# Head norms, gain factors and gate tiles of the query-key-value stage, rearranged

## The chip, the cores and the metric

The kernel is one program on one core of a Trainium2 chip. The core has five engines with an instruction queue each: TensorE (PE; its weight loads are listed as PEld), VectorE (DVE), ScalarE (ACT), GpSimd (POOL) and SyncE (SP), which here only starts transfers. Each queue is worked off in order, and an instruction that has to wait holds back all that stands behind it. The metric is the device time of one launch in microseconds (us), the median of several runs. "Faster" and "slower" are against the kernel before.

## The reference

A trunk of two layers on x (1024 tokens, width 1024, all float32): layer 0 is RWKV-7 time mixing and an MLP; from its output shared keys, values and forget gates are made; layer 1 is causal attention with 16 heads of 64 and an MLP. The part that the change touches is this one:

```
def shared_kv(x, kv_norm_g, kv_w, kv_f_bias, k_norm_g):
    h = rmsnorm(x, kv_norm_g)
    proj = h @ kv_w                                   # keys | values | 16 forget logits
    k = to_heads(proj[..., :D]); v = to_heads(proj[..., D:2 * D])
    f_logit = (proj[..., 2 * D:] + kv_f_bias)
    k = rmsnorm(k, k_norm_g)                          # per head, 64 wide
    c = cumsum(log_sigmoid(f_logit))
...
    q = rmsnorm(to_heads(h @ w_q), q_norm_g)          # h = rmsnorm(x, attn_norm_g)
    logits = q k^T / 8 + (c[t] - c[s]);  causal softmax;  p v;  @ w_o
```

## The kernel before, in words

**Where the stage stands.** `stage_qkv` follows the first MLP and runs in the profile from about 1393 us to 1676 us; `stage_attention` follows it. The normalised x is kept feature-first in blocks of 512 features by 512 tokens (B11, B21 for the first 512 tokens, B12, B22 for the others). The norm gains `kv_norm_g` and `attn_norm_g` are multiplied into the rows of the weights (`scale_on`, L72, called at L1579). Each float32 operand is split into a high and a low part (`wh`/`wl` for weights, `xh`/`xl` for x), and three products of parts make one float32 product.

**Six jobs of 512 output columns.** Keys, queries and values of the lower 512 columns, then of the upper 512. The first job (keys) is done plainly: for each half of the tokens, 96 matmuls into four banks of PSUM (`plain`), then `leave` copies the four banks to two tiles C on ScalarE. The other five jobs go through `proj_seven`, a Strassen-Winograd scheme with seven products A11, A12, S1, S2, S3, A22, S4 of 48 matmuls each. It needs sums of x blocks (T1 to T4, formed in place over the raw blocks B11 and B21 in `Operands.forms` and `forms2`, on VectorE with casts on ScalarE) and sums of weight blocks (`form`). Four of the seven products give a tile C, 512 tokens by 256 columns.

**What follows a C.** For keys and queries, `heads_T(...).emit` first makes the head norms: on ScalarE a square (`hsq`, L1675), on VectorE a sum over 64 (`hss`, L1676), then `rsqrt_small` (L79 to L91: VectorE, two steps on ScalarE, four on VectorE, on small tiles of 128x16), then a multiplication of C in place (L1680). The four transposes and their way to memory (`turn`, L1683: transpose on TensorE, `ht` with the head gain on ScalarE at L1690, a store from SP at L1691) come later: `emit` puts `turn` in the list `later` with a count of 4, and `tick()`, called once per product, lets it run when the count is used up. `tick(2)` between the two halves of the plain job takes two off the first half's count.

**Buffers.** PSUM has eight banks, all with the tag `mm`: a product of `proj_seven` takes two, a group of the plain job four, one `turn` two. C has three places, `ht` two, each part of weights (`wh`, `wl`) four.

**Attention.** Heads go in pairs. For each pair, `load` fetches keys and queries (`raw`), the cumulated gates of two heads spread over all partitions (`b<-d_c`, L1899, three places), and GpSimd makes of each a masked copy (`dg`, L1914, pool `t_d` with three places). `scores` (L1804, L1808, VectorE) adds `dg` and `b` to the products of TensorE and takes the row extreme; ScalarE then takes the exponential.

**What sets the order.** The framework's scheduler writes out one static order per engine from the program's order, priorities and a model of times; a tile can be placed in memory as soon as what lay there is done with. So an edit here can move instructions that it doesn't name.

Of the kernel before, what the change touches and what calls it, by code (L numbers as in the profile page):

```python
# [8 lines left out]
F32 = mybir.dt.float32  # L9
F32R = mybir.dt.float32r  # L10
AF = mybir.ActivationFunctionType
ALU = mybir.AluOpType
AX = mybir.AxisListType
# [3 lines left out]
P = 128  # L17
# [3 lines left out]
N = 64  # L21
NK = D // P
C = 64
# [29 lines left out]
    "q": {"n0": "vvvv", "n1": "vvsvvvvv", "r": "ssssssssssssssss", "Bh": "vvvvvvvv", "Bl": "vpvpvpvp", "t1": "ppvv",  # L53
        "t2": "vvvv", "t3": "vpvv", "t4": "vvvv", "T1h": "ssss", "T1l": "pppp", "T2h": "ssss", "T2l": "vpvv", "T3h":
        "spvv", "T3l": "vpvp", "T4h": "ssss", "T4l": "vpvp", "B22h": "vsss", "B22l": "vvpp", "wh": "spspsssssssvss",
        "wl": "vpvpvpvvvvpvpv", "wf": "pvvvvpvv", "wg": "vvvpvvsvvvvvssss"},
}


# [12 lines left out]
def scale_on(k, e, out, x, col):  # L72
    if e == "s":
        k.nc.scalar.mul(out, x, col)
    else:
        engine(k, e).tensor_scalar(out, x, col, None, op0=ALU.mult)
# [1493 lines left out]
def proj_seven(k, ps, p0, p1, p2, pool, w_tile, tick, X, w, gain, emit, number):  # L1570

    nc = k.nc
    A = {}
    for h in range(2):
        t = w_tile()
        nc.sync.dma_start(t, w[512 * h:512 * h + 512].rearrange("(k p) e -> p k e", p=P))
        for i in range(NK // 2):
            g = gain[:, 4 * h + i:4 * h + i + 1]
            scale_on(k, ENG["q"]["wg"][8 * number + 4 * h + i] if number < 2 else "v", t[:, i], t[:, i], g)  # L1579
        A[f"A1{h + 1}"], A[f"A2{h + 1}"] = t[:, :, 0:256], t[:, :, 256:512]  # L1580

    def form(dst, x, y, op):
        e = ENG["q"]["wf"][4 * number + "S1 S2 S3 S4".split().index(an)] if number < 2 else "v"
        engine(k, e).tensor_tensor(A[dst], A[x], A[y], op=op)

    U, V = (p2.tile([P, 2, 512], F32, tag=t, name=t, bufs=1) for t in ("U", "V"))
    for q, (an, bn) in enumerate([("A11", "B11"), ("A12", "B21"), ("S1", "T1"), ("S2", "T2"), ("S3", "T3"),
                                  ("A22", "T4"), ("S4", "B22")]):
        if an == "S1":
            A["S"] = pool().tile([P, NK // 2, 256], F32, tag="S", name="S", bufs=1)  # L1590
            form("S", "A21", "A22", ALU.add)
        elif an == "S2":
            form("S", "S", "A11", ALU.subtract)
        elif an == "S3":
            form("A21", "A11", "A21", ALU.subtract)
        elif an == "S4":
            form("S", "A12", "S", ALU.subtract)
        src = A[an if an[0] == "A" else "A21" if an == "S3" else "S"]
        wh, wl = (p.tile([P, NK // 2, 256], F32R, tag=t, name=t, bufs=4) for p, t in ((p0, "wh"), (p1, "wl")))
        es = (ENG["q"]["wh"][7 * number + q], ENG["q"]["wl"][7 * number + q]) if number < 2 else ("s", "vp"[q % 2])  # L1600
        split(k, None, src, None, *(engine(k, e) for e in es), dst=(wh, wl))
        o = [ps.tile([P, 512], F32, tag="mm", name="mm") for _ in range(2)]
        for t in range(4):
            ts = slice(t * P, t * P + P)
            for i in range(NK // 2):
                xh, xl = X[bn][i]
                for m, (x, y) in enumerate(((xh, wh), (xh, wl), (xl, wh))):
                    k.pe.matmul(o[t // 2][:, 256 * (t % 2):256 * (t % 2) + 256], x[:, ts], y[:, i],
                                     start=t % 2 == 0 and i == 0 and m == 0,
                                     stop=t % 2 == 1 and i == NK // 2 - 1 and m == 2)  # L1610
        C = None if an in ("A11", "S1", "S2") else pool().tile([P, 2, 512], F32, tag="C", name="C", bufs=3)
        for b in range(2):
            if an == "A11":
                nc.scalar.copy(U[:, b], o[b])
            elif an == "S1":
                nc.scalar.copy(V[:, b], o[b])
            elif an == "S2":
                nc.vector.tensor_tensor(U[:, b], U[:, b], o[b], op=ALU.add)
                nc.gpsimd.tensor_tensor(V[:, b], V[:, b], U[:, b], op=ALU.add)
            else:  # L1620
                nc.vector.tensor_tensor(C[:, b], (V if an in ("S3", "S4") else U)[:, b], o[b], op=ALU.add)
            if an == "S3":
                nc.vector.tensor_tensor(U[:, b], U[:, b], o[b], op=ALU.add)
        tick()
        if C is not None:
            emit(*{"A12": (0, 0), "S3": (1, 1), "A22": (1, 0), "S4": (0, 1)}[an], C)
# [20 lines left out]
def stage_qkv(k, a, xt, xs, raw, p0, W, late):  # L1647
    nc, tc, ps = k.nc, k.tc, k.ps
    with ExitStack() as ctx:
# [3 lines left out]
        pool, wn, later = None, 2, []  # L1653
# [12 lines left out]

        def heads_T(dst, gcol, f0):

            def emit(fh, th, Cb):
                with tc.high_priority(offset=PRIO):  # L1670
                    ss = sp.tile([P, 2, 8], F32, tag="hss", name="hss")
                    o3 = [Cb[:, b].rearrange("p (h n) -> p h n", n=N) for b in range(2)]
                    for b in range(2):
                        sq = pool.tile([P, 8, N], F32, tag="hsq", name="hsq", bufs=1)
                        nc.scalar.activation(sq, o3[b], AF.Square)  # L1675
                        nc.vector.tensor_reduce(ss[:, b], sq, axis=AX.X, op=ALU.add)  # L1676
                    rs = sp.tile([P, 2, 8], F32, tag="hrs", name="hrs")
                    rsqrt_small(k, sp, rs, ss, 1.0 / N, 1e-6)
                    for b in range(2):
                        nc.vector.tensor_tensor(o3[b], o3[b], rs[:, b].unsqueeze(2).broadcast_to([P, 8, N]), op=ALU.mult)  # L1680

                def turn():
                    for j in range(2):  # L1683
# [5 lines left out]
                        t = pool.tile([P, 512], F32, tag="ht", name="ht")  # L1689
                        nc.scalar.mul(t, tp, gcol[:, f // P:f // P + 1])  # L1690
                        nc.sync.dma_start(dst[f:f + P, 512 * th:512 * th + 512], t)  # L1691
                later.append([4, turn])
            return emit

        def tokens(dst, f0):
# [16 lines left out]
        w, gain, emit = jobs.pop(0)  # L1712
# [10 lines left out]
        wl, U = None, p2.tile([P, 2, 512], F32, tag="U", name="U", bufs=1)  # L1723
# [13 lines left out]
                                    stop=h == 1 and i == NK // 2 - 1 and n == 2)  # L1737

        def leave(th, o):
            C = [pool.tile([P, 2, 512], F32, tag="C", name="C", bufs=3) for _ in range(2)]  # L1740
            for t in range(4):
                for fh in range(2):
                    nc.scalar.copy(C[fh][:, t // 2, 256 * (t % 2):256 * (t % 2) + 256], o[t][:, 256 * fh:256 * fh + 256])
            for fh in range(2):
                emit(fh, th, C[fh])
        o = [mm("mm") for _ in range(4)]
        plain(0, 0, o)
        X.second(xt, lambda: mm("tp"))
# [6 lines left out]
        o = [mm("mm") for _ in range(4)]  # L1755
# [12 lines left out]
def stage_attention(k, a, op):  # L1768
# [3 lines left out]
    wo = op.tile([P, D], F32, name="aw")  # L1772
    with ExitStack() as ctx:
        lp, pp, vp, dp, bp, kp, kk = (ctx.enter_context(tc.tile_pool(name="t_" + n, bufs=b, reuse_waits="tile"))
                                      for n, b in (("l", 4), ("p", 2), ("v", 2), ("d", 3), ("b", 3), ("k", 2), ("kk", 2)))
        sp = ctx.enter_context(tc.tile_pool(name="t_s", bufs=6, reuse_waits="tile"))
        ps_s = ctx.enter_context(tc.tile_pool(name="t_ps", bufs=2, space=PSUM, reuse_waits="tile"))
        ps_t = ctx.enter_context(tc.tile_pool(name="t_pt", bufs=3, space=PSUM, reuse_waits="tile"))
# [313 lines left out]
```

## Time and profile before

| what | value |
|---|---|
| median of 3 runs | 2641.9 us (2640.52 to 2645.92) |
| profiled execution | 2639.1 us, of which the span from first to last instruction is 2637.4 us |
| TensorE busy / VectorE busy / ScalarE busy | 96% / 70% / 47% of the span |
| granted TensorE clock, mean | 0.983 |

A row of the timeline has start, length, engine, line, operation, output<-input, shape and count; in square brackets the idle time of the engine just before it and who ended it. A row of the windows has the stretch, its length, then busy time and count of instructions per engine, the granted clock of TensorE as a share of the full one, the share of the transfer engines and the rate.

### The profile page before, as it was taken

How to read it: one execution, taken by the hardware profiler on the slowest of the kernel's cores; microseconds unless marked ns; L12 is line 12 of the kernel's file. 1: busy time of each engine (PE TensorE's matmuls, PEld its weight loads, DVE VectorE, ACT ScalarE, POOL GpSimd, SP SyncE). 2: the span in 40 equal slices, each digit the busy share in tenths (PEclk: the TensorE clock that was granted, in tenths of full speed). 3: DMA queues.
4: the chain of work that ended last, by engine and by line, in shares of the span. 5: the costliest groups of instructions: out<-in, count | busy, mean ns of one | idle time of the engine just before them, and what ended most of it. 6: DMA issues, size and time to landing. Idle time of an engine off the chain costs nothing.

```text
span 2637.4 us, 44718 instructions
## 1 busy us (share of the span) xinstructions
PE 2537.5 (96%) x17601; PEld 2141.5 (81%) x17601; DVE 1852.2 (70%) x2982; ACT 1237.6 (47%) x2136; POOL 507.5 (19%) x395
## 2 busy tenths in 40 slices
PE   7999998799999999999999899999999999999999
PEld 4887897677778888888888899887887888878887
DVE  6665965788868777566778768587736877746675
ACT  4763324422355555443455424588715555543332
POOL 2011222866620000000301122344300000000020
PEclk9999999899999999999999999999999999999999
DMA  4468654966425544666641321755341644376664
GB/s 129 126 168 189 169 131 145 231 162 164 114 66 164 169 139 160 250 227 240 229 147 65 118 76 64 209 137 148 87 152 48 208 163 144 131 264 220 224 212 141
DMA packets 413510, 417.51 MB, mean 158 GB/s; under 512 B 189482, under 2 KB 297218, under 8 KB 413300
## 3 DMA queue, kind: packets, MB, share of 16 engines
q1 hardware_dynamic: 394068, 392.50, 49.0%
q0 software_dynamic: 4128, 12.66, 1.3%
q10 hardware_dynamic: 15104, 9.51, 1.2%
q8 instruction: 138, 2.26, 0.4%
q14 instruction: 72, 0.59, 0.1%
HBM read 292.76 MB, written 121.82 MB: 157 GB/s over the span
## 4 chain that ended last, share of the span: by engine, by line
PE 69%; DVE 15%; DMA 6%; issue 4%; ACT 3%; POOL 2%; SPq 1%; POOLq 0%; DVEq 0%; ACTq 0%
PE mm L365 34%; PE mm L768 7%; PE mm L766 7%; PE mm L767 7%; PE mm L824 4%; PE tp L368 2%; PE wo L365 1%; DVE Tb L316 1%; DMA b<-d_c 1%; PE s L365 1%; DVE Tm L314 1%; PE z1p L1001 1%; DVE AE L427 1%; PE o L365 1%; DMA R<-d_sm 1%
## 5 line engine op out<-in xcount | busy, mean ns | idle before, releaser
L365 PE MATMUL mm<-ol,oh 128*128 128x512 f32 x896 | 349.9, 391 | 1.3 <-DVE ol L733 1.3
L365 PE MATMUL mm<-oh 128*128 128x512 f32 x896 | 349.7, 390 | 1.3 <-ACT oh L730 1.3
L365 PE MATMUL mm<-oh,ol 128*128 128x512 f32 x896 | 349.9, 390 | 0.5 <-DVE ol L733 0.3
L730 ACT CAST oh<-ra 128x1024 fp32r<-128x1024 f32 x108 | 113.8, 1054 | 335.8 <-PE mm L365 237.5
L733 DVE TENSOR_TENSOR ol<-ra,oh 128x1024 fp32r<-128x1024 f32 x108 | 137.8, 1276 | 123.6 <-ACT oh L730 123.4
L365 PEld LDWEIGHTS mm<-ol,oh 128*128 128x128 f32 x896 | 168.9, 188 | 36.9 <-DVE ol L733 1.7
L365 PEld LDWEIGHTS mm<-oh,ol 128*128 128x128 f32 x896 | 168.9, 188 | 36.5 <-DVE ol L733 1.4
L365 PEld LDWEIGHTS mm<-oh 128*128 128x128 f32 x896 | 168.8, 188 | 36.5 <-ACT oh L730 1.7
L766 PE MATMUL mm<-xhT,ah 128*128 128x512 f32 x448 | 174.3, 389 | 0.0
L767 PE MATMUL mm<-xlT,ah 128*128 128x512 f32 x448 | 174.3, 389 | 0.0
L768 PE MATMUL mm<-xhT,al 128*128 128x512 f32 x448 | 174.3, 389 | 0.0
L1495 POOL DMA_DIRECT2D xt<-d_xh x8 | 4.4, 552 | 755.1 <-DMA rb<-in_mlp_w_out_dram 421.4
L730 ACT CAST ah<-w 128x512 fp32r<-128x512 f32 x128 | 79.3, 621 | 113.5 <-PE mm L767 102.1
L766 PE MATMUL mm<-xhB,ah 128*128 128x512 f32 x336 | 130.7, 389 | 0.0
L767 PE MATMUL mm<-xlB,ah 128*128 128x512 f32 x336 | 130.7, 389 | 0.0
L768 PE MATMUL mm<-xhB,al 128*128 128x512 f32 x336 | 130.7, 389 | 0.0
L733 DVE TENSOR_TENSOR ol<-rb,oh 128x1024 fp32r<-128x1024 f32 x92 | 120.8, 1313 | 2.1 <-ACT oh L730 1.8
L1811 ACT ACTIVATE l<-l,mx 128x512 f32<-128x512 f32 (+7 forms) x128 | 99.2, 776 | 34.3 <-DVE mx L1808 34.1
L1268 ACT ACTIVATE z<-z 128x512 f32<-128x512 f32 x112 | 70.8, 633 | 68.9 <-DVE z L1265 67.3
L767 PEld LDWEIGHTS mm<-xlT,ah 128*128 128x128 f32 x448 | 84.1, 188 | 17.6
L730 ACT CAST oh<-rb 128x1024 fp32r<-128x1024 f32 x92 | 96.4, 1048 | 4.0 <-DMA rb<-in_mlp_w_out_dram 4.0
L768 PEld LDWEIGHTS mm<-xhT,al 128*128 128x128 f32 x448 | 84.1, 188 | 17.4
(487 smaller groups left out, 6952.6 us busy)
## 6 DMA issues: line engine op xcount, KB each, us to landing
rb<-in_mlp_w_out_dram SPq DMA_DIRECT2D x124, 512.0 KB
ra<-d_H SPq DMA_DIRECT2D x108, 512.0 KB
w<-in_mlp_w_in_dram SPq DMA_DIRECT2D x64, 512.0 KB
d_H<-z SPq DMA_DIRECT2D x56, 512.0 KB
d_H<-sums SPq DMA_DIRECT2D x32, 768.0 KB
raw<-in_rwkv_w_rkv_dram SPq DMA_DIRECT2D x24, 512.0 KB
KRz<-d_KR SPq DMA_DIRECT2D x16, 512.0 KB
KRz<-d_BK SPq DMA_DIRECT2D x16, 512.0 KB
```

The source lines that it names most:

```text
L314: nc.vector.tensor_tensor(Tm[:, :, 0:n, 0:m], Nb[:, :, j, j + 1:32].unsqueeze(3).broadcast_to(S), Tb[:, :, j:j + 1, 0:m].broadcast_to(S), ...
L316: nc.vector.tensor_tensor(Tb[:, :, j + 1:32, 0:m], Tb[:, :, j + 1:32, 0:m], Tm[:, :, 0:n, 0:m], op=ALU.add)
L365: return self.tc.keep_in_program_order(self.tc.nc.tensor.matmul(*args, **kw))
L368: return self.tc.keep_in_program_order(self.tc.nc.tensor.transpose(*args))
L730: nc.scalar.copy(hi, src)
L733: lo_eng.tensor_tensor(lo, src, hi.bitcast(F32), op=ALU.subtract)
L766: te.matmul(out, ah, bh, start=i == 0, stop=False)
L767: te.matmul(out, ah, bl, start=False, stop=False)
L768: te.matmul(out, al, bh, start=False, stop=i == n - 1)
L824: nc.tensor.matmul(o[e][half], wt[:, i % 4, es], xs[i][part][:, 512 * half:512 * half + 512], start=i == 0 and wt is hi and part == 0, sto ...
L1268: nc.scalar.activation(x, x if o is None else o, AF.Relu)
L1811: nc.scalar.activation(l, l, AF.Exp, bias=m, scale=-1.0, accum_out=SM[:, j, qb:qb + 1])
```

## The change

1. **One root for two C.** In the plain job the head norms of the two C of a token half are made together: `norm([C0, C1])` with tiles of 128x32 and one `rsqrt_small`, where there were two of 128x16. It is called from `leave`; `emit` then only files the turns.
2. **C over a raw block.** The two C of the second token half lie no longer in the pool of C but in one tile with the tag `KRz0`, the place of raw block B11, which is free once the form T3 has been split.
3. **Later turns.** The turns of the plain job get the counts 5 (first half) and 6 (second half) in place of 4.
4. **Gain factors on ScalarE.** All factors of weights run on ScalarE: the four of job 2's first half and the eight of each of the jobs 3 to 6, 36 in all, leave VectorE. Four were on ScalarE already.
5. **Gates' places.** The pool `t_d` of attention has four places in place of three, which also shifts what lies behind it in memory, the tiles `b` among it.

What it does to the order is shown at three places. First, TensorE after the plain job. xhB_13663 is block B21 (product A12); in the first piece, of before, xhT_13938 is T1 (product S1).

```order
L365 MATMUL mm<-wh,xhB_13663 128x256
L365 MATMUL mm<-wl,xhB_13663 128x256
L365 MATMUL mm<-wh,xlB_13664 128x256
L368 MATMUL tp<-ident,C 128x128 x16
L365 MATMUL mm<-wh,xhT_13938 128x256
L365 MATMUL mm<-wl,xhT_13938 128x256
L365 MATMUL mm<-wh,xlT_13939 128x256
```

In the change's order xhT_13927 is T1 and xhT_13935 is T2 (product S2):

```order
L365 MATMUL mm<-wh,xhT_13927 128x256
L365 MATMUL mm<-wl,xhT_13927 128x256
L365 MATMUL mm<-wh,xlT_13928 128x256
L368 MATMUL tp<-ident,C 128x128 x16
L365 MATMUL mm<-wh,xhT_13935 128x256
L365 MATMUL mm<-wl,xhT_13935 128x256
L365 MATMUL mm<-wh,xlT_13936 128x256
```

The sixteen transposes of the first half move one product back. Those of the second half stood after S2; they stand now after A22, two products later, in one group of 24 with the eight of product A12.

Second, VectorE where the second half's C are multiplied (L1680 before, L1681 now). Of before, twelve rows from factors of a later job's weights on; the last multiplication that the transposes need follows five rows further down. L1584 is a weight sum, L1621 and L1618 take products out of PSUM:

```order
L76 TENSOR_SCALAR w<-w,cols_443 128x512 x4
L1676 TENSOR_REDUCE hss<-hsq 128x8
L733 TENSOR_TENSOR wl<-S,wh 128x1024
L88 TENSOR_TENSOR rs_t<-rs_v,hrs 128x16
L1618 TENSOR_TENSOR U<-U,mm 128x512
L1676 TENSOR_REDUCE hss<-hsq 128x8
L1584 TENSOR_TENSOR S<-w 128x1024
L89 TENSOR_TENSOR rs_t<-rs_t,hrs 128x16
L85 TENSOR_SCALAR rs_v<-hss 128x16
L1618 TENSOR_TENSOR U<-U,mm 128x512
L1584 TENSOR_TENSOR w<-w 128x4x256
L90 TENSOR_SCALAR rs_t<-rs_t 128x16
```

Now:

```order
L1621 TENSOR_TENSOR C<-U,mm 128x512
L1677 TENSOR_REDUCE hss<-hsq 128x8
L88 TENSOR_TENSOR rs_t<-rs_v,hrs 128x32
L89 TENSOR_TENSOR rs_t<-rs_t,hrs 128x32
L90 TENSOR_SCALAR rs_t<-rs_t 128x32
L91 TENSOR_TENSOR hrs<-hrs,rs_t 128x32
L1677 TENSOR_REDUCE hss<-hsq 128x8
L1681 TENSOR_TENSOR C<-C,hrs 128x512 x4
L85 TENSOR_SCALAR rs_v<-hss 128x16
L733 TENSOR_TENSOR wl<-S,wh 128x1024
L1584 TENSOR_TENSOR S<-w 128x1024
L1618 TENSOR_TENSOR U<-U,mm 128x512
```

The factors are gone from VectorE, and the multiplication of the second half's C stands ahead of the next job's weight sum; before, its last part stood behind it.

Third, SP ahead of attention. Of before, from the last stores of the values (`d_v<-C`):

```order
L1698 DMA d_v<-C 128x4x256
L1893 DMA raw<-d_r 64x1024
L1899 DMA b<-d_c 128x1024 x2
L1901 DMA V<-d_v 128x8x128
L1698 DMA d_v<-C 128x4x256
L1899 DMA b<-d_c 128x1024
L1901 DMA V<-d_v 128x8x128
L1927 DMA aw<-in_attn_w_o_dram 128x1024
```

Now the same loads (L1909) stand ahead of the last six stores of queries and of all `raw`:

```order
L1696 DMA d_k<-ht 128x512 x6
L1696 DMA d_r<-ht 128x512 x2
L1909 DMA b<-d_c 128x1024 x3
L1696 DMA d_r<-ht 128x512
L1704 DMA d_v<-C 128x4x256
L1696 DMA d_r<-ht 128x512
L1903 DMA raw<-d_k 64x1024 x4
```

The three gate loads go from the end of the stage's transfers to a place ahead of sixteen loads of keys and queries. On GpSimd, on the other hand, nothing of this stage moves.

The diff:

```
@@ table ENG, stage "q" @@
-        "wl": "vpvpvpvvvvpvpv", "wf": "pvvvvpvv", "wg": "vvvpvvsvvvvvssss"},
+        "wl": "vpvpvpvvvvpvpv", "wf": "pvvvvpvv", "wg": "ssssssssssssssss"},
@@ proj_seven @@
-            scale_on(k, ENG["q"]["wg"][8 * number + 4 * h + i] if number < 2 else "v", t[:, i], t[:, i], g)
+            scale_on(k, ENG["q"]["wg"][8 * number + 4 * h + i] if number < 2 else "s", t[:, i], t[:, i], g)
@@ stage_qkv, heads_T @@
-            def emit(fh, th, Cb):
+            def norm(Cs):
                 with tc.high_priority(offset=PRIO):
-                    ss = sp.tile([P, 2, 8], F32, tag="hss", name="hss")
-                    o3 = [Cb[:, b].rearrange("p (h n) -> p h n", n=N) for b in range(2)]
-                    for b in range(2):
+                    n = len(Cs)
+                    o3 = [C[:, b].rearrange("p (h n) -> p h n", n=N) for C in Cs for b in range(2)]
+                    ss = sp.tile([P, 2 * n, 8], F32, tag=f"hss{n}", name="hss")
+                    for o, s in zip(o3, range(2 * n)):
                         sq = pool.tile([P, 8, N], F32, tag="hsq", name="hsq", bufs=1)
-                        nc.scalar.activation(sq, o3[b], AF.Square)
-                        nc.vector.tensor_reduce(ss[:, b], sq, axis=AX.X, op=ALU.add)
-                    rs = sp.tile([P, 2, 8], F32, tag="hrs", name="hrs")
-                    rsqrt_small(k, sp, rs, ss, 1.0 / N, 1e-6)
-                    for b in range(2):
-                        nc.vector.tensor_tensor(o3[b], o3[b], rs[:, b]..., op=ALU.mult)
+                        nc.scalar.activation(sq, o, AF.Square)
+                        nc.vector.tensor_reduce(ss[:, s], sq, axis=AX.X, op=ALU.add)
+                    rs = sp.tile([P, 2 * n, 8], F32, tag=f"hrs{n}", name="hrs")
+                    rsqrt_small(k, sp, rs, ss, 1.0 / N, 1e-6, tag=f"{n}")
+                    for o, s in zip(o3, range(2 * n)):
+                        nc.vector.tensor_tensor(o, o, rs[:, s]..., op=ALU.mult)
+
+            def emit(fh, th, Cb, wait=4, normed=False):
+                if not normed:
+                    norm([Cb])
...
-                later.append([4, turn])
+                later.append([wait, turn])
+            emit.norm = norm
@@ stage_qkv, leave @@
-            C = [pool.tile([P, 2, 512], F32, tag="C", name="C", bufs=3) for _ in range(2)]
+            if th:
+                C2 = k.rz.tile([P, 2, 2, 512], F32, tag="KRz0", name="C")
+            C = [C2[:, fh] if th else pool.tile([P, 2, 512], F32, tag="C", name="C", bufs=3) for fh in range(2)]
...
+            emit.norm(C)
             for fh in range(2):
-                emit(fh, th, C[fh])
+                emit(fh, th, C[fh], 5 + th, True)
@@ stage_attention @@
-                      for n, b in (("l", 4), ("p", 2), ("v", 2), ("d", 3), ("b", 3), ("k", 2), ("kk", 2)))
+                      for n, b in (("l", 4), ("p", 2), ("v", 2), ("d", 4), ("b", 3), ("k", 2), ("kk", 2)))
```

More of the change, by code (lines that the diff above doesn't have):

```diff
@@ L1667, in heads_T @@
         def heads_T(dst, gcol, f0):
-            def emit(fh, th, Cb):
+            def norm(Cs):
                 with tc.high_priority(offset=PRIO):
-                    ss = sp.tile([P, 2, 8], F32, tag="hss", name="hss")
-                    o3 = [Cb[:, b].rearrange("p (h n) -> p h n", n=N) for b in range(2)]
-                    for b in range(2):
+                    n = len(Cs)
+                    o3 = [C[:, b].rearrange("p (h n) -> p h n", n=N) for C in Cs for b in range(2)]
+                    ss = sp.tile([P, 2 * n, 8], F32, tag=f"hss{n}", name="hss")
+                    for o, s in zip(o3, range(2 * n)):
                         sq = pool.tile([P, 8, N], F32, tag="hsq", name="hsq", bufs=1)
-                        nc.scalar.activation(sq, o3[b], AF.Square)
-                        nc.vector.tensor_reduce(ss[:, b], sq, axis=AX.X, op=ALU.add)
-                    rs = sp.tile([P, 2, 8], F32, tag="hrs", name="hrs")
-                    rsqrt_small(k, sp, rs, ss, 1.0 / N, 1e-6)
-                    for b in range(2):
-                        nc.vector.tensor_tensor(o3[b], o3[b], rs[:, b].unsqueeze(2).broadcast_to([P, 8, N]), op=ALU.mult)
+                        nc.scalar.activation(sq, o, AF.Square)
[3 more added lines that the diff above has]
+                    for o, s in zip(o3, range(2 * n)):
+                        nc.vector.tensor_tensor(o, o, rs[:, s].unsqueeze(2).broadcast_to([P, 8, N]), op=ALU.mult)
+            def emit(fh, th, Cb, wait=4, normed=False):
+                if not normed:
+                    norm([Cb])
                 def turn():
```

## The prediction, made before the changed kernel ran

> **What bounds the kernel now.** I read the page's busy shares first, then the windows by stage, then the rows of TensorE that have idle time.
>
> ```profile
> span 2637.4 us, 44718 instructions
> PE 2537.5 (96%) x17601; PEld 2141.5 (81%) x17601; DVE 1852.2 (70%) x2982; ACT 1237.6 (47%) x2136; POOL 507.5 (19%) x395
> ```
>
> TensorE is busy for 96% of the span, so only what lets it stand still, or slows its clock, can be won. In windows over the stage of the change and the start of attention (stretch, length, then busy time of PE, PEld, DVE, ACT, POOL; then granted clock):
>
> ```profile
> 1410.00:1430.00 20.00, 20.00 (x90) 16.55 (x89) 20.00 (x26) 10.56 (x20) 0.00 (x0) 1.00 0.00 1
> 1430.00:1450.00 20.00, 20.00 (x128) 18.21 (x127) 19.90 (x28) 11.67 (x22) 5.74 (x2) 1.00 0.00 1
> 1450.00:1470.00 20.00, 16.41 (x138) 15.93 (x136) 18.47 (x32) 11.62 (x23) 3.63 (x2) 1.00 0.53 178
> 1470.00:1490.00 20.00, 15.40 (x118) 15.09 (x119) 15.25 (x29) 6.01 (x11) 4.52 (x2) 0.83 0.09 34
> 1490.00:1510.00 20.00, 20.00 (x170) 20.00 (x169) 15.41 (x26) 8.69 (x16) 4.36 (x2) 1.00 0.26 87
> 1680.00:1710.00 30.00, 27.74 (x236) 23.79 (x236) 23.65 (x81) 23.28 (x56) 11.44 (x7) 0.89 0.57 169
> 1710.00:1911.00 201.00, 191.55 (x1897) 164.61 (x1894) 156.75 (x519) 157.13 (x398) 81.88 (x45) 1.00 0.46 123
> ```
>
> VectorE is full from 1410 to 1450 us while TensorE is full too; then TensorE falls short by 8.2 us from 1450 to 1490, and VectorE is the engine that is behind. ScalarE is at about half all along. From 1490 on TensorE is full again. TensorE's rows with idle time, and one ahead of them (in brackets: the wait before the row and who ended it):
>
> ```profile
> 1451.90 1.03 PE L368 MATMUL tp<-ident,C 128*128 128x128 f32 x8
> 1453.79 1.09 PE L368 MATMUL tp<-ident,C 128*128 128x128 f32 x8 [0.85 <-ACT ht L1690]
> 1474.60 2.15 PE L368 MATMUL tp<-ident,C 128*128 128x128 f32 x8 [7.34 <-DVE C L1680]
> 1676.77 0.94 PE L365 MATMUL s<-K,Q 128*128 128x512 f32 x4 [0.18 <-DVE C L1621]
> 1680.70 1.05 PE L365 MATMUL s<-K,Q 128*128 128x384 f32 x4 [2.99 <-DVE mx L1804]
> 1683.11 1.83 PE L365 MATMUL s<-K,Q 128*128 128x384 f32 x4 [1.36 <-DVE mx L1804]
> ```
>
> The first three stand in the stage of the change: transposes of the plain job's C, without a wait, waiting for a free bank (0.85) and for the last multiplication of C (7.34). The others are the start of attention. After the long waits the clock is down (windows of TensorE alone: busy, granted clock, transfers):
>
> ```profile
> 1475.00:1477.00 2.00, 2.00 (x11) 0.50 0.00 0
> 1477.00:1479.00 2.00, 2.00 (x16) 0.85 0.68 257
> 1682.00:1684.00 2.00, 0.89 (x3) 0.60 1.11 370
> 1684.00:1686.00 2.00, 2.00 (x9) 0.50 0.80 280
> 1686.00:1688.00 2.00, 2.00 (x10) 0.50 0.08 31
> 1688.00:1690.00 2.00, 2.00 (x12) 0.69 0.00 0
> ```
>
> So each stall costs its own length and, behind it, some us of work at half speed.
>
> **The change part by part.** *Later turns.* A product of 48 matmuls takes 5.75 us:
>
> ```profile
> 1507.70 5.75 PE mm L365 x48
> ```
>
> The second half's transposes go from behind S2 to behind A22, 2 x 5.75 = 11.5 us of TensorE's work later; the wait for them is 7.34 us. That alone covers it, if VectorE does not come later than now. What VectorE does before that point:
>
> ```profile
> 1457.34 1.68 DVE L76 TENSOR_SCALAR w<-w,cols 128x512 f32<-128x512 f32 x4 [0.19 <-DMA w<-in_kv_w_dram]
> 1471.29 1.23 DVE L90 TENSOR_SCALAR rs_t<-rs_t 128x16 f32<-128x16 f32 x1
> 1473.86 1.29 DVE L1680 TENSOR_TENSOR C<-C,hrs 128x512 f32<-128x512 f32 x2
> L76 DVE TENSOR_SCALAR w<-w,cols 128x512 f32<-128x512 f32 x36 | 15.6, 494 | 8.4 <-DMA w<-in_kv_w_dram 4.5 <-DMA w<-in_attn_w_q_dram 3.1 <-ACT xhT L69 0.7
> L90 DVE TENSOR_SCALAR rs_t<-rs_t 128x16 f32<-128x16 f32 x16 | 9.9, 618 | 0.3
> L74 ACT ACTIVATE w<-w,cols 128x512 f32<-128x512 f32 x4 | 2.6, 714 | 5.7 <-DMA w<-in_attn_w_q_dram 5.7
> ```
>
> *Gain factors.* Sixteen of the 36 factors (four groups) stand ahead of that multiplication: 4 x 1.68 = 6.7 us that VectorE no longer has there. *One root.* Two of the four root chains of the plain job go; the three middle steps of a chain are tiny but take up to 1.23 us when GpSimd is at work (618 ns mean), so 1 to 3 us more. And the multiplication now stands ahead of the weight sums L1584 that wait for a later job's weights. VectorE should have the second half's C done near 1460 us, and TensorE, unstalled, comes for them at 1451.9 (end of A12, before the first turns) + 1.8 (first turns) + 4 x 5.75 = 1476.7: some 16 us of slack. Of the 24 transposes the last eight need product A12's C. Its root now stands on ScalarE behind four factors that wait for weights:
>
> ```profile
> 1455.88 0.44 SPq L1576 DMA_DIRECT2D w<-in_kv_w_dram  x1
> 1462.91 1.28 DVE L76 TENSOR_SCALAR w<-w,cols 128x512 f32<-128x512 f32 x3 [0.51 <-DMA w<-in_kv_w_dram]
> ```
>
> These land at 1462.9, ScalarE takes 2.6, and VectorE then has a weight sum, two copies, the root's rest and C, about 6 us: 1472, needed at 1478.5. 6 us of slack. Gain of the long wait: 7.34.
>
> *C over the raw block.* Now the second half's copies out of PSUM wait for a C place, held by the first half until its transposes:
>
> ```profile
> 1442.60 1.21 DVE L1164 TENSOR_TENSOR xlT<-raw,xhT 128x1024 fp32r<-128x1024 f32 x1
> 1453.64 1.18 ACT L1743 COPY C<-mm 128x256 f32<-128x256 f32 x4
> 1458.83 1.27 ACT L1690 ACTIVATE ht<-tp,cols 128x512 f32<-128x512 f32 x2 [2.90 <-DMA d_k<-ht]
> ```
>
> They come at 1453.64, 13 us after the plain job's last matmul (1451.9 - 2 x 5.75 = 1440.4), and hold four of eight banks; that is the 0.85. Over KRz0 they can run once T3 is split, at 1443.8 now (first row), so the banks are free when S1 wants them. Gain 0.85. The third row is a price of the other sign: `ht` has two places, and a third `ht` waits 2.9 us for a store. The group of 24 makes six `ht` in a row, so ScalarE can stand twice for some 3 us; behind it stand casts of weights, which run up to four products (23 us) ahead, and squares whose C are wanted three products later. I put it at 0; without that cover it is 2 x 2.9 = 5.8.
>
> *The clock behind it.* 2 us at 0.50, 2 at 0.85 and 0.4 us before them at half: 1.0 + 0.3 + 0.2 = 1.5. Sum of the stage: 7.34 + 0.85 + 1.5 = 9.7, between 0 and 9.7. The other factors (20 of 36, in jobs 4 to 6) and the longer time on ScalarE (36 x 714 = 25.7 us where VectorE took 36 x 494 = 17.8) lie beside a TensorE that is full; 0 both ways unless ScalarE becomes the bound (below).
>
> *Gates' places.* What the first scores wait for:
>
> ```profile
> 1628.11 18.47 SPq L1691 DMA_DIRECT2D d_r<-ht  x3
> 1671.92 2.48 SPq L1899 DMA_DIRECT2D b<-d_c  x2
> 1678.25 1.10 POOL L1914 TENSOR_SCALAR_AFFINE_SELECT dg<-b 128x1024 f32<-128x1024 f32 x1 [9.00 <-DMA b<-d_c]
> 1680.67 1.09 POOL L1914 TENSOR_SCALAR_AFFINE_SELECT dg<-b 128x1024 f32<-128x1024 f32 x1 [1.32 <-DMA b<-d_c]
> 1675.93 0.69 DVE L1621 TENSOR_TENSOR C<-V,mm 128x512 f32<-128x512 f32 x1 [2.19 <-PE mm L365]
> 1679.38 0.29 DVE L1804 CUSTOM_DVE_ANT_0 l<-s,dg 128x128 f32<-128x128 f32 x1 [2.76 <-POOL dg L1914]
> 1681.79 0.29 DVE L1804 CUSTOM_DVE_ANT_0 l<-s,dg 128x128 f32<-128x128 f32 x1 [1.24 <-POOL dg L1914]
> ```
>
> The loads are issued at 1671.9, land six to eight us later, GpSimd waits 9.00 for them, and VectorE and TensorE behind it. In the new order they stand between the stores of the row at 1628, so about 1630 to 1647, 25 us earlier; GpSimd is free for `dg` from 1669.2 (1678.25 - 9.00). Then VectorE starts when it has the last C out, 1676.6, not at 1679.38, and does the two heads without the pause, 1.2 us each (1681.79 - 1.24 - 1679.38): 1679.0. TensorE's second four of unit two start at 1679.1, not 1683.11: 4.0 us. The clock, if it holds, gives back 0.9 x 0.4 + 4 x 0.5 + 2 x 0.31 = 3.0, but VectorE has 23.65 us of work in the 30 us after 1680, against 78% later (156.75 of 201), so it would become the bound; I take half, 1.5. Sum 5.5, between 0 (loads late all the same) and 7.0. [...]
>
> **The sum.** 9.7 + 5.5 = 15.2. The profiled execution took 2639.1 (span 2637.4 and 1.7 around it): 2623.9. The median of the runs is 2.8 above it: 2641.9 - 15.2 = 2626.7, so **2627**.
>
> **The rivals.** *The start of attention stays* (chance 0.11): another late load (V, the last keys) ends last in place of the gates; for it, the transfer engines are full at 1682 (1.11). Against it, keys and queries of the first pair are loaded before. 2641.9 - 9.7 = 2632. *The stage's wait only moves* (0.11): the group of 24 waits for A12's C, or for banks, as long as before, and only attention gains: 2641.9 - 5.5 = 2636. Against it stand the 6 us of slack. *Both stay* (0.11): a gain under 5 us, 2639; also the case that the change doesn't do what it says. *ScalarE becomes the bound* (0.07), on the slower side: in each half job it now waits in its queue for weights (VectorE's 8.4 us of waits move to it) and then needs 2.6 us, nine lumps of about 3.5 us, with copies out of PSUM behind them. If TensorE finds the banks full each time, 9 x 3.5 = 31 us come in and 2641.9 - 15.2 + 31 = 2658; it decides from five lumps of nine on (17 us against 15.2). Against it: 11.62 of 20 us busy, a product lasts 5.75, and its banks are wanted again only three products on. [...]
>
> **How the numbers follow.** The forecast holds 0.60. Its own spread, 2622 to 2631, is the bounds of its terms (2641.9 - 16.7 = 2625) and the spread of three runs (2640.5 to 2645.9). To leave out no more than 2 in 10 it must take in the first two rivals: **2621 to 2637**. A difference under 0.2% (5.3 us) can't be told from none: faster 0.60 + 0.11 + 0.11 = 0.82, same 0.11, slower 0.07.
>
> **What would show it.** Right: no row of TensorE with over 1 us of idle time between 1440 and 1490, clock 1.00 in its windows, the 24 transposes in one piece; VectorE below 18 of 20 us from 1430 to 1450; `b<-d_c` issued before the first `raw`, `dg` without a wait for it, the first scores' gaps under 0.5 us. Wrong: transposes that wait for C or `ht`, matmuls that wait for ScalarE's copies, a gap of over 2 us at the first scores with another load as its end.

## The result, and the profile after

| | before | changed |
|---|---|---|
| median of 6 runs, us | 2641.83 | 2624.64 |
| profiled execution's span, us | 2637.4 | 2621.6 |
| first matmul of the stage to first scores, us | 282.82 | 272.45 |
| first scores to the fourth group of `o<-pt,V` (32 matmuls), us | 28.53 | 22.97 |

The changed kernel is faster: ratio 0.9937, 95% interval 0.9917 to 0.9957, so 17.2 us between the medians; 2627 was forecast. Two executions far off all others, one of `gates_only` (6393 us) and one of `turns_and_gates` (3571 us), are in no ratio of this document. The last two rows are differences of start times: 1392.91, 1675.73 and 1704.26 us in the trace of before, and in that of the changed kernel those of these rows:

```profile
1393.54 0.39 PE L365 MATMUL mm<-wh,xhB 128*128 128x512 f32 x1
1665.99 0.86 PE L365 MATMUL s<-K,Q 128*128 128x512 f32 x4
1688.96 1.97 PE L365 MATMUL o<-pt,V 128*64 128x128 f32 x32
```

In the profiled executions the stage of queries and keys gave 10.4 us and the start of attention 5.6; the span is 15.8 shorter, since the stage began 0.6 later and all that follows is 0.5 shorter. The changed kernel's page:

```profile
span 2621.6 us, 44704 instructions
PE 2531.6 (97%) x17601; PEld 2135.2 (81%) x17601; DVE 1837.4 (70%) x2936; ACT 1260.4 (48%) x2168; POOL 508.4 (19%) x395
```

Its windows over the same stretches (length, busy PE, PEld, DVE, ACT, POOL, then granted clock, transfers):

```profile
1430.00:1450.00 20.00, 20.00 (x124) 18.03 (x123) 17.53 (x23) 13.26 (x24) 5.20 (x2) 1.00 0.00 1
1450.00:1470.00 20.00, 20.00 (x171) 20.00 (x170) 18.01 (x29) 13.27 (x24) 6.13 (x3) 1.00 0.46 158
1470.00:1490.00 20.00, 20.00 (x171) 20.00 (x171) 18.63 (x34) 12.06 (x21) 5.06 (x3) 1.00 0.21 79
```

TensorE is full from 1430 to 1490 and its clock whole, where before it lacked 8.2 us and the clock fell to 0.83. VectorE is still at 18 of 20 us there from 1450 on. Rows of the timeline, engine by engine: the turns of the plain job, the two multiplications of C that the second group needs, ScalarE's last copies of the second half and an `ht` that waits, then the gates' loads, `dg`, and the first scores:

```profile
1458.62 1.91 PE L368 MATMUL tp<-ident,C 128*128 128x128 f32 x16
1477.63 2.78 PE L368 MATMUL tp<-ident,C 128*128 128x128 f32 x24
1457.83 2.49 DVE L1681 TENSOR_TENSOR C<-C,hrs 128x512 f32<-128x512 f32 x4
1468.41 2.39 DVE L1681 TENSOR_TENSOR C<-C,hrs 128x512 f32<-128x512 f32 x2
1442.05 0.65 ACT L1752 COPY C<-mm 128x256 f32<-128x256 f32 x2
1481.64 1.33 ACT L1695 ACTIVATE ht<-tp,cols 128x512 f32<-128x512 f32 x2 [0.49 <-DMA d_k<-ht]
1628.92 1.28 SPq L1909 DMA_DIRECT2D b<-d_c  x3
1659.46 2.15 POOL L1924 TENSOR_SCALAR_AFFINE_SELECT dg<-b 128x1024 f32<-128x1024 f32 x2
1667.02 0.94 PE L365 MATMUL s<-K,Q 128*128 128x512 f32 x4 [0.18 <-DVE C L1621]
1668.32 2.16 PE L365 MATMUL s<-K,Q 128*128 128x384 f32 x8 [0.35 <-DVE mx L1814]
1672.47 0.33 PE L368 MATMUL tp<-ident,l 128*128 128x128 f32 x1 [1.00 <-ACT pt L1838]
```

The 24 transposes start without a wait, 17.3 us after the second half's C are done (1457.83 + 2.49 = 1460.32), and run in one piece. The second half's last copies out of PSUM start at 1442.05, not at 1453.64. The gates' loads are issued 37 us ahead of the first scores (1665.99), where before it was 4 us; `dg` has no wait for them, and the two gaps of 2.99 and 1.36 us at the first scores have become 0.35. A new short wait has come, 1.00 us for the copy of `pt`.

### The profile page after: what moved, and what is told of

Its sections match the earlier page's. It is cut to its first block, busy times and chain, and to the rows that moved or that the text cites. A ratio compares the mean times of both kernels' runs of the same rounds, so it can differ in the third digit from the quotient of the medians.

```text
span 2621.6 us, 44704 instructions
## 1 busy us (share of the span) xinstructions
PE 2531.6 (97%) x17601; PEld 2135.2 (81%) x17601; DVE 1837.4 (70%) x2936; ACT 1260.4 (48%) x2168; POOL 508.4 (19%) x395
## 4 chain that ended last, share of the span: by engine, by line
PE 76%; DVE 11%; DMA 4%; issue 4%; ACT 3%; POOL 1%; SPq 1%; ACTq 0%; POOLq 0%; DVEq 0%
PE mm L365 38%; PE mm L767 7%; PE mm L766 7%; PE mm L768 7%; PE mm L824 5%; PE tp L368 2%; PE wo L365 2%; PE s L365 1%; PE o L365 1%; PE z1p L1001 1%; DVE Tm L314 1%; DVE Tb L316 1%; DMA b<-d_c 1%; DVE AE L427 1%; PE sums L201 1%
## 5 line engine op out<-in xcount | busy, mean ns | idle before, releaser
L766 PEld LDWEIGHTS mm<-xhT,ah 128*128 128x128 f32 x448 | 84.1, 188 | 17.4
```

Of the source, the lines that this page charges most:

```text
L766: te.matmul(out, ah, bh, start=i == 0, stop=False)
```

## The experiments

All ratios are to the kernel before, timed beside it, with 95% intervals. "Stage" and "start" are the two stretches of the table above, from each run's own trace. Where the long wait is there, the stage scatters: 282.82, 284.27 and 284.08 us in three kernels with the same order in it. Where neither it nor a wait for a bank of PSUM is left, the stage lies between 272.1 and 273.0 in six kernels; with the later turns alone, where waits for a bank stay, it is 274.5. Without the gates' edit the start lies between 26.3 and 28.5, though these kernels were not changed there: a difference of 2 us in the start isn't the gates' edit by itself.

| run | ratio | stage | start |
|---|---|---|---|
| gates_only | 0.9979 (0.9971 to 0.9988) | 284.27 | 22.97 |
| room_without_fourth_gate | 0.9983 (0.9972 to 0.9993) | 284.08 | 22.97 |
| all_but_gates | 0.9956 (0.9943 to 0.9970) | 272.45 | 26.47 |
| factors_only | 0.9994 (0.9983 to 1.0006) | 281.87 | 27.14 |
| raw_place_only | 1.0005 (0.9996 to 1.0015) | 284.54 | 27.14 |
| raw_place_and_factors | 0.9959 (0.9947 to 0.9971) | 272.44 | 26.31 |
| turns_only | 0.9965 (0.9953 to 0.9978) | 274.45 | 26.53 |
| all_but_later_turns | 0.9935 (0.9923 to 0.9947) | 272.44 | 22.95 |
| factors_back_on_vector | 0.9967 (0.9955 to 0.9979) | 279.84 | 23.04 |
| turns_and_gates | 0.9962 (0.9948 to 0.9975) | 274.51 | 22.95 |
| early_factors | 0.9942 (0.9931 to 0.9954) | 273.00 | 22.97 |
| scalar_load_doubled | 0.9946 (0.9934 to 0.9957) | 272.12 | 22.96 |

### Gates: the places, or the memory behind them

`gates_only` puts the one edit of attention into the kernel before, `room_without_fourth_gate` gives the place to another pool ahead of the gates' ones, and `all_but_gates` takes the edit out of the changed kernel.

```
gates_only, in the kernel before:
-("l", 4), ("p", 2), ("v", 2), ("d", 3), ("b", 3)
+("l", 4), ("p", 2), ("v", 2), ("d", 4), ("b", 3)
room_without_fourth_gate, in the kernel before:
-("l", 4), ("p", 2), ("v", 2), ("d", 3), ("b", 3)
+("l", 5), ("p", 2), ("v", 2), ("d", 3), ("b", 3)
all_but_gates, in the changed kernel:
-("d", 4), ("b", 3)
+("d", 3), ("b", 3)
```

> The kernel before with one edit: the pool of dg has four places. Theory (places move the loads): b<-d_c is issued ahead of all loads of keys and queries, dg has no wait for it, the first scores' waits fall from 2.99 + 1.36 to under 0.5 us, the clock after them stays at 1.00, and the time is 5.5 to 7 us shorter (ratio about 0.9975); the stage of queries and keys keeps its waits of 7.34 and 0.85. Rival (start of attention stays, another load ends last): the waits move to V or to raw, 0 to 2 us.

> The kernel before with a fifth place in the pool l of attention (which lies ahead of the gates' pools in memory) and three places of dg as before. Theory (what counts is where the tiles b lie, since the written order has the loads b<-d_c ahead of the keys here too): as with the fourth dg, no wait of dg, 5 to 6 us shorter (ratio 0.998). Rival (the fourth dg place itself counts): first scores' waits as before, ratio 1.000.

> The changed kernel with three places of dg again. Theory (two separate gains that add): the stage of queries and keys has no wait of TensorE, as in the changed kernel, and the first scores wait 2.99 + 1.36 as before; 9.7 to 10.5 us shorter than before (ratio 0.996). Rival (the two are one chain, since a stage that ends 10 us earlier meets the gates' loads 10 us less ready): the first scores' waits grow, and under 5 us are left.

Both first edits make the start 22.97 us long, as in the changed kernel, and both are some 5 us faster. In the second there are still three `dg`; so it isn't the fourth `dg` that counts. What both have is that the loads of `b` are issued ahead of all `raw`, where before they stood behind them, at 1671.92. Of `room_without_fourth_gate`, rows of SP:

```profile
1647.81 1.27 SPq L1899 DMA_DIRECT2D b<-d_c  x3
1656.91 3.01 SPq L1893 DMA_DIRECT2D raw<-d_k  x4
```

In both runs these loads wait once, for 9.7 us, for a matmul of the stage. The explanation is that the tiles `b`, moved by one place, come to lie on memory that is free earlier. It fits both edits, but no view shows addresses, so it is argued and not shown. Waits of TensorE from 1390 to 1700 us in `gates_only` (engine, line, who ended them: us in total, times, longest):

```profile
PE tp L368 <- DVE C L1680: 7.8, 1, 7.8
...
PE s L365 <- DVE mx L1804: 0.4, 1, 0.4
```

The stage keeps its long wait and the first scores lose theirs. `all_but_gates` is the mirror of it: the stage is 272.45 long, as in the changed kernel to the hundredth, and the first scores wait. But they wait in one gap of 3.23 us, not in two of 2.99 and 1.36, and the start is 2.1 us shorter than before; so the two gains add to within 2 us, and the rival of one common chain falls.

### One cause or two: factors, raw place, turns

"Factors" is part 4 of the change, "raw place" part 2 (C over a raw block) and "turns" part 3. The prediction read the wait of 7.34 us as VectorE's lateness. `factors_only` takes 6.7 us of work from it, `turns_only` wants the transposes later.

```
factors_only, in the kernel before:
-"wg": "vvvpvvsvvvvvssss"
+"wg": "ssssssssssssssss"
-scale_on(k, ENG["q"]["wg"][8 * number + 4 * h + i] if number < 2 else "v", t[:, i], t[:, i], g)
+scale_on(k, ENG["q"]["wg"][8 * number + 4 * h + i] if number < 2 else "s", t[:, i], t[:, i], g)
turns_only, in the kernel before:
-def emit(fh, th, Cb):
+def emit(fh, th, Cb, wait=4):
-later.append([4, turn])
+later.append([wait, turn])
-emit(fh, th, C[fh])
+emit(fh, th, C[fh], 5 + th)
```

> The kernel before with one edit: all gain factors on ScalarE. Theory (VectorE's lateness is a sum of parts, and the factors are 6.7 us of it): the wait of 7.34 us for C shrinks to 2 to 4 us, since the copies of the second half out of PSUM still wait for a place of C until the first turns; the wait for a bank of 0.85 stays; 4 to 7 us shorter. Rival one (the factors alone are the cause): no wait is left, 9 us shorter. Rival two (ScalarE as the bound): 10 to 30 us longer, with matmuls that wait for ScalarE's copies.

> The kernel before with one edit: counts 5 and 6 for the turns of the plain job. The prediction said of this part that it alone covers the wait of 7.34 us, as the transposes are wanted 11.5 us later. By that: 8 to 9.7 us shorter. Rival, worked out now from the order: the first half holds its two C one product (5.75 us) longer, the copies of the second half out of PSUM wait for them, and so the second half's C are ready some 5 us later too; a wait of 2 to 5 us stays and the wait for banks grows; 2 to 6 us shorter.

`factors_only` won nothing: all three expectations missed. One window of this run, with VectorE in the third place of busy time, then its longest wait of TensorE, then rows of ScalarE and VectorE:

```profile
1450.00:1470.00 20.00, 16.40 (x138) 15.93 (x136) 11.16 (x14) 15.86 (x29) 4.92 (x3) 1.00 0.48 159
```

```profile
PE tp L368 <- DVE C L1680: 6.6, 1, 6.6
```

```profile
1453.62 1.18 ACT L1743 COPY C<-mm 128x256 f32<-128x256 f32 x4
1457.51 2.56 ACT L74 ACTIVATE w<-w,cols 128x512 f32<-128x512 f32 x4 [1.60 <-DMA w<-in_kv_w_dram]
1461.19 0.69 DVE L1676 TENSOR_REDUCE hss<-hsq 128x8 f32<-128x512 f32 x1 [4.41 <-ACT hsq L1675]
1473.01 1.28 DVE L1680 TENSOR_TENSOR C<-C,hrs 128x512 f32<-128x512 f32 x2
```

VectorE falls from 18.47 to 11.16 us busy of 20, and TensorE still waits 6.6 us for it. Now VectorE itself waits, 4.41 us for a square, which stands on ScalarE behind the second half's last copies (not before 1453.62, when a place of C is free) and behind factors that wait for weights. So there is a chain that starts late, whatever VectorE has to do, and part of the work taken from VectorE now stands in the same chain on ScalarE.

`turns_only` does what the prediction said of it: no wait for C, the stage 8.4 us shorter. Its rival had the right mechanism and the wrong end: of this run, rows of the turns and of the multiplications of C:

```profile
1459.10 0.66 PE L368 MATMUL tp<-ident,C 128*128 128x128 f32 x4 [0.24 <-ACT V L1616]
1460.63 1.09 PE L368 MATMUL tp<-ident,C 128*128 128x128 f32 x8 [0.88 <-ACT ht L1690]
1473.62 1.28 DVE L1680 TENSOR_TENSOR C<-C,hrs 128x512 f32<-128x512 f32 x2
1478.56 1.29 DVE L1680 TENSOR_TENSOR C<-C,hrs 128x512 f32<-128x512 f32 x2
1478.83 3.14 PE L368 MATMUL tp<-ident,C 128*128 128x128 f32 x24
```

The second half's C are done at 1474.9 and wanted at 1478.83, 4 us of slack and not 16. A12's are done at 1479.85, while the group runs; its seventeenth transpose, the first that needs them, starts at 1480.77, so 0.9 us of slack is left. The group takes 3.14 us where it takes 2.78 in the changed kernel, and 0.27 of that is a wait of this transpose's weight load for a bank (`ht`). The other waits for a bank are still there too, 0.24 + 0.88: the second half leaves PSUM late, its last copies standing at 1460.47.

The next two runs put the other causes to the test: the raw place alone, and all of the change but the later turns.

```
raw_place_only, in the kernel before:
-C = [pool.tile([P, 2, 512], F32, tag="C", name="C", bufs=3) for _ in range(2)]
+if th:
+    C2 = k.rz.tile([P, 2, 2, 512], F32, tag="KRz0", name="C")
+C = [C2[:, fh] if th else pool.tile([P, 2, 512], F32, tag="C", name="C", bufs=3) for fh in range(2)]
all_but_later_turns, in the changed kernel:
-emit(fh, th, C[fh], 5 + th, True)
+emit(fh, th, C[fh], 4, True)
```

> The kernel before with one edit: the two C of the second half lie over the raw block B11. Theory now (after the factors alone won nothing): the wait of 7.34 us is the end of a chain that starts late, when the first turns free a place of C and the second half leaves PSUM at 1453.6; the chain then starts 13 us earlier and the wait shrinks by several us, though VectorE's written order still puts the last root behind factors that wait for weights at 1462.9, so 3 to 6 us of it may stay; the wait for a bank (0.85) goes; 2 to 6 us shorter. Rival (the start of the chain is the only cause): no wait left, 9.7 us shorter. Rival (VectorE's load is the cause): 0.85 alone, 1 us shorter.

> The changed kernel with the counts of the turns back at 4, so that the second half's transposes stand behind S2 again and are wanted near 1465 us. In the changed kernel's trace the second half's C are done at 1460.3. Theory: no wait; the time of the changed kernel within 1 us (ratio to before 0.9937). Rival (later turns are what does it, as the run with them alone suggests): a wait of 4 to 7 us comes back, ratio 0.996 to 0.997.

`raw_place_only` won nothing either, where 2 to 6 us were expected. The wait for a bank is gone, but TensorE's wait for C is now two waits, the first of them, 3.3 us, for the first half's C. Of this run that line of the waits, then of its timeline the second half leaving PSUM and the steps of its last root on VectorE:

```profile
PE tp L368 <- DVE C L1680: 8.2, 2, 4.9
```

```profile
1443.23 1.75 ACT L1745 COPY C<-mm 128x256 f32<-128x256 f32 x6
1461.13 0.17 DVE L85 TENSOR_SCALAR rs_v<-hss 128x16 f32<-128x16 f32 x1
1462.95 1.66 DVE L76 TENSOR_SCALAR w<-w,cols 128x512 f32<-128x512 f32 x4
...
1468.62 1.26 DVE L89 TENSOR_TENSOR rs_t<-rs_t,hrs 128x16 f32<-128x16 f32 x1
...
1474.18 1.29 DVE L1680 TENSOR_TENSOR C<-C,hrs 128x512 f32<-128x512 f32 x2
```

The copies come 10 us earlier, the end does not: the root takes 13 us, from 1461.13 to the multiplication at 1474.18. Its two steps on ScalarE are through at 1465.15; then factors, weight sums and sums into U stand ahead of and between its four small steps in VectorE's order. `all_but_later_turns`, on the other hand, has the whole gain; of its timeline, the second half's multiplication and transposes:

```profile
1457.73 2.50 DVE L1681 TENSOR_TENSOR C<-C,hrs 128x512 f32<-128x512 f32 x4
1466.01 1.91 PE L368 MATMUL tp<-ident,C 128*128 128x128 f32 x16
```

The C are done at 1460.2 and wanted at 1466.0. So later turns aren't needed beside the rest; the theory held. Is it, then, the two parts that are worth nothing alone?

```
raw_place_and_factors: both edits, of factors_only and of raw_place_only, in the kernel before
factors_back_on_vector: the changed kernel with "wg" and the "v" of before
```

> The kernel before with two edits that won nothing alone: the second half's C over the raw block, and the factors on ScalarE; counts of 4, a root for each C, three dg. Theory (two causes side by side, each of which alone lets the second half's C end near 1473: the late start of the chain, and VectorE's queue with the last root behind factors that wait for weights): with both gone the C are done near 1462 and wanted near 1465 to 1467, so 0 to 1 us of wait is left: 8 to 10 us shorter, ratio 0.9965. Rival (the single root is needed too, since two root chains take VectorE's small steps one behind the other): 3 us or more of wait stays, ratio 0.998 to 1.000.

> The changed kernel with the 36 factors back on VectorE. Theory (the factors are worth nothing here): the second half's C are done 8 to 13 us later, at 1468 to 1473, wanted at 1477.6: no wait, the time of the changed kernel within 1 us (ratio 0.9937). Rival (the factors are what makes room for C): a wait of 2 to 7 us, ratio 0.995 to 0.997.

Of `raw_place_and_factors`, the second half's last multiplication and its transposes:

```profile
1464.88 1.29 DVE L1680 TENSOR_TENSOR C<-C,hrs 128x512 f32<-128x512 f32 x2
1469.64 1.91 PE L368 MATMUL tp<-ident,C 128*128 128x128 f32 x16
```

C are done at 1466.17 and wanted at 1469.64, so there is no wait; the stage is 10.4 us shorter, all that the changed kernel has there. Nothing alone, everything together: two causes stood side by side, and either one by itself kept the end near 1475 (1473.01 + 1.28 and 1474.18 + 1.29). Neither the single root nor the later turns is needed. These four kernels (neither edit, each alone, both) show it. Without the factors, though, the rest loses much; of `factors_back_on_vector`, rows of the timeline and TensorE's line of the waits:

```profile
1445.00 0.65 ACT L1752 COPY C<-mm 128x256 f32<-128x256 f32 x2 [3.10 <-DVE xlT L1164]
1468.71 0.88 DVE L76 TENSOR_SCALAR w<-w,cols 128x512 f32<-128x512 f32 x2 [2.44 <-DMA w<-in_kv_w_dram]
1480.19 4.63 DVE L1681 TENSOR_TENSOR C<-C,hrs 128x512 f32<-128x512 f32 x4
1483.68 3.25 PE L368 MATMUL tp<-ident,C 128*128 128x128 f32 x14 [2.25 <-DVE C L1681]
```

```profile
PE tp L368 <- DVE C L1681: 3.8, 3, 2.2
```

The theory said 8 to 13 us later and no wait, and it missed; the rival's wait came. C are done at 1484.8, which is 21 us later than in the changed kernel (1460.3, and this run's stage began 3.2 later), and TensorE stands for 3.8 us and then works at half clock (0.50 in its window from 1484 to 1486). The factors' own time, four groups of 1.68 by the rows of before, is 6.7 us of these 21; they also wait for weights in VectorE's queue (2.44), and ScalarE's copies wait for VectorE to split T3 (3.10). That this kernel's stage is even longer than with the turns alone (279.84 against 274.45) may come from the single root, with which both C of a half end behind the last square, or from the raw place; no run separates them.

`turns_and_gates` asks whether the other three parts add anything to these two.

```
turns_and_gates: both edits, of turns_only and of gates_only, in the kernel before
```

> The kernel before with two edits: the counts 5 and 6 of the turns, and four places of dg. Theory (the two gains add; the stage was 8.4 us shorter with the turns alone, and the start of attention 5.6 with the gates alone): 14 us shorter, ratio 0.9947, 2 us above the changed kernel, which are the waits for banks at the first turns. Rival (the other three parts are worth nothing beside these): the time of the changed kernel, 0.9937. Rival (with the last C of the group just in time, a shift brings its wait back): 0.996 to 0.998.

By the trace the two gains add, 8.3 + 5.6. Of the 2 us to the changed kernel 1.1 are the first turns' waits for a bank and 0.4 the longer group of 24, and the rest isn't accounted for; the clock is 1.00 in the whole stage, and no wait for C is there. The timed ratio, 0.9962, doesn't bear this out: the expected 0.9947 lies just outside its interval, and 0.996 to 0.998 was the rival's, a wait that comes back. The profiled execution, at 2626.2 us the fastest of the five that count, shows no such wait; what the others have isn't recorded. How far this kernel is above the changed one stays open.

### What the factors cost ScalarE, and which of them count

```
early_factors, in the changed kernel:
-... if number < 2 else "s", t[:, i], t[:, i], g)
+... if number < 2 else "s" if number < 4 else "v", t[:, i], t[:, i], g)
scalar_load_doubled, in the changed kernel, behind each factor:
+nc.scalar.copy(t[:, i], t[:, i])
```

> The changed kernel with the sixteen factors of the last two jobs back on VectorE, so that only those of the jobs 2 to 4 run on ScalarE. Theory (the later ones lie beside a TensorE that is full, as the prediction put at 0): the time of the changed kernel, ratio 0.9937 within 0.001. Rival (they count too): 0.995 to 0.997, with waits of TensorE for C or U after 1510.

> The changed kernel with a copy of the same part of weights in place on ScalarE behind each of the 40 factors, which changes no value and adds 40 times some 0.6 us, 24 us, to ScalarE in the stage. Theory (ScalarE has room: 13 of 20 us busy in the windows of the changed kernel): the time of the changed kernel within 2 us, ratio 0.9937 to 0.9945. Rival (ScalarE becomes the bound, lumps of 5 us and more with copies out of PSUM behind them): 10 us or more above the changed kernel, ratio 0.997 and more, with matmuls that wait for ScalarE's copies.

Groups of ScalarE from 1400 to 1670 us in `scalar_load_doubled` (busy, mean ns | idle time before them):

```profile
L74 ACT ACTIVATE w<-w,cols 128x512 f32<-128x512 f32 x36 | 23.3, 717 | 3.6 <-DMA w<-in_kv_w_dram 3.6
L1580 ACT COPY w<-w 128x512 f32<-128x512 f32 x36 | 20.7, 621 | 0.0
```

Some 21 us more on ScalarE change nothing in the stage (272.12 against 272.45), and sixteen factors back on VectorE next to nothing (273.00); both ratios' intervals hold the changed kernel's 0.9937. ScalarE, busy for 157 of the 270 us from 1400 to 1670 in this run, isn't the bound, and the later factors lie beside a full TensorE.

No run points to a version that is faster than the changed kernel by more than these measurements can tell; `all_but_later_turns` equals it.

## Why the prediction was right, step by step

- **Sum and place: right, the sum with some luck.** 9.7 + 5.5 forecast; 10.4 + 5.6 in the trace, so the stage gave 0.7 more than the prediction's own upper bound, and where that lies was not followed up. The sum is that of the waits and the clock behind them, and it comes out whichever part takes the waits away; the shares of the parts below did not come out. Every sign named ahead came: no row of TensorE with a wait between 1440 and 1490, clock 1.00, 24 transposes in one piece, VectorE at 17.53 of 20 from 1430 to 1450, `b<-d_c` ahead of `raw`, gaps of 0.18 and 0.35 at the first scores. The C of the second half and of A12 were put near 1460 and 1472; they came at 1460.3 and 1470.8.
- **"That alone covers it" (later turns): right in the result, by luck in the margin.** The run with them alone has no wait for C, but 4 us of slack in place of 16 for the second half and 0.9 in place of 6 for A12: the copies out of PSUM wait for the first turns, which moved as well. The condition that the prediction set, that VectorE does not come later, failed for A12's C by some 2.5 us (1478.56 against 1475.47, stage start 0.6 later).
- **"VectorE is the engine that is behind": the step that failed.** It was read from a busy share of 18 to 20 us and from the name that ended the wait. `factors_only` took 7 us out of the window and the wait stayed at 6.6. What ended late was a chain: place of C, copies, square, sum, root, with ScalarE's queue in it. Beside it VectorE's order was a second cause. So the price of the *gain factors*, 4 x 1.68 = 6.7 us, was not a term that adds: it is 0 alone, and beside the other four parts the factors move the end by 21 us.
- **The raw place, 0.85: right as a term, too small as a part.** The wait for a bank is gone with it alone and stays without it (0.88 in `turns_only`). But together with the factors it removes the 7.34 as well, which the prediction gave to the turns. It gave one wait to one part, while two sets of parts each suffice.
- **One root, 1 to 3 us: not seen.** The stage is as short without it (272.44 in `raw_place_and_factors`). The small steps that the prediction put at up to 1.23 us take up to 2.40 in the trace of before.
- **`ht` at 0: right.** Of two waits for `ht` stores feared at 2.9 each, ScalarE has one of 0.5 near the group of 24, and TensorE doesn't see it.
- **Gates, 4.0 + 1.5: sum right, split off.** The gaps of TensorE shrink by 3.0 (0.18 + 2.99 + 1.36 before, 0.18 + 0.35 + 1.00 after, the 1.00 being the new wait for `pt`), and the other 2.6 of the 5.6, what is left, are put down to work that is no longer done at half clock (0.50 in the windows of before from 1684 to 1688). The forecast took half of 3.0 for the clock, arguing that VectorE would become the bound; it didn't, and the clock is 1.00 in every window of the changed kernel from 1660 to 1700; in the trace of before it had fallen at the first scores (0.60 from 1682 to 1684) with no gap over 2.99 us. The 7.0 that the prediction worked out for the start with a whole clock didn't come, partly for the wait of 1.00 that came in.
- **Rivals.** ScalarE as the bound fell in `scalar_load_doubled`. The start of attention stayed in no run that moved the gates. "The stage's wait only moves" is what happens when the factors stay on VectorE: in `factors_back_on_vector` the group of 24 does wait.

## What to carry to other kernels

Before an engine is called behind because a wait ends with it, look at the wait's whole chain: which places, which queue and which load its first member waited for; taking 7 us of work from the busy engine was worth nothing here (`factors_only`, 0.9994) while a second chain ended at the same time. Parts that win nothing alone can win everything together, and a part that covers alone can be redundant, so an edit's gain isn't a sum of its parts' prices. And when a pool gets one place more, look at what moves behind it in memory and in the order of the loads: here a place more in another pool won as much as the fourth `dg`.

## What the runs showed of the hardware that was not expected

The price of a stall in TensorE's clock came in steps in these runs. Windows of TensorE alone (busy, granted clock, transfers): of `raw_place_only`, whose gaps of 3.33 and 4.92 us end at 1455.15 and 1475.02; of `gates_only`, whose gap of 7.85 us ends at 1476.27; and of the kernel before, whose gap of 7.34 us ends at 1474.60:

```profile
1454.00:1456.00 2.00, 0.85 (x4) 0.71 0.64 226
1458.00:1460.00 2.00, 2.00 (x18) 0.94 1.00 350
...
1475.00:1476.00 1.00, 0.88 (x4) 0.66 0.00 0
```

```profile
1470.00:1472.00 2.00, 0.00 (x0) 0.82 0.71 262
...
1480.00:1482.00 2.00, 2.00 (x13) 0.62 0.35 130
```

```profile
1470.00:1472.00 2.00, 0.00 (x0) 0.69 0.17 62
...
1476.00:1478.00 2.00, 2.00 (x13) 0.60 0.27 103
```

The windows between two edges read 1.00 or 0.50 (0.50 in all four of `gates_only` from 1472 to 1480). The edges that follow are estimates worked out from the windows above, on the reading that the clock is at one of these two values: a mean of 0.71 over 2 us then says 1.16 us at half. So in the first run it falls at 1454.84 and rises at 1458.24, 3.40 us, and falls again at 1475.32, six times 3.41 after the first fall. In the second it is at half from 1471.28 to 1481.52, three times 3.41; in the third from 1470.76 to 1477.6, twice 3.42. So in these three executions the edges lie on a grid of 3.41 us, by this estimate. The length of a gap alone doesn't tell when the clock falls: from the gap's start to the fall it is 2.86 us in `gates_only`, 3.50 in the kernel before, and 3.02 and 5.22 in `raw_place_only`; at the first scores of before it fell with no gap over 2.99 us. The author's reading, which no run was made to test, is that the work in a stretch of the grid counts. Worked back from these edges, the clock fell after a stretch with 31% of work (the first scores before, 1679.0 to 1682.4, with 1.05 us of work in it) and not after one with 47% (`raw_place_only`, 1468.5 to 1471.9); it rose after 87% (before, 1474.2 to 1477.6) and not after 54% (`gates_only`, 1474.7 to 1478.1). Nearly the same long wait cost 1.5 us of clock in one execution (7.34, before) and 2.6 in another (7.85, `gates_only`), each half of the work from the gap's end to the rise; the reading puts that down to where the wait lies against the grid. Of the 1.45 us by which the stage of `gates_only` is longer than before, in the same order, 1.1 are of this kind; the wait itself is 0.5 longer.

VectorE's multiplications of C show the other surprise. In the changed kernel four of them take 2.49 us (1457.83, above), and the four of the first half 4.71; beside these GpSimd was at work:

```profile
1444.34 4.71 DVE L1681 TENSOR_TENSOR C<-C,hrs 128x512 f32<-128x512 f32 x4
1444.51 2.79 POOL L733 TENSOR_TENSOR wl<-S,wh 128x1024 fp32r<-128x1024 f32 x1 [2.27 <-ACT wh L730]
```

GpSimd has no instruction from 1456.6 to 1460.3. The small steps of the roots show the same, without an exception, in the stage of both kernels (1400 to 1670 us): the 22 steps of 128x16 or 128x32 that took 0.66 to 2.40 us ran beside a GpSimd instruction for over 90% of their time, and the other 128 took at most 0.19. No run moved GpSimd's work away, so that it is what stretches VectorE's, and how, is not shown.
